# TensorE's instructions of both attention pipelines stay in the program's order

## The chip, the cores and the metric

The kernel runs on one core of a Trainium2 chip. The metric is the device time of one execution in microseconds (us). Five engines share the work: TensorE (PE, matmuls; PEld is its weight load), VectorE (DVE), ScalarE (ACT), GpSimd (POOL) and SyncE (SP, which issues most of the transfers).

## What is computed

Two layers of a hybrid backbone over 512 latent and 256 context tokens, model width 1024, all in float32. Each layer's mixer has three branches, merged by gates and projected:

```python
y_f = fourier_mix(f)
y_na = neighbourhood_attention(q, k, v, k_ctx, v_ctx, rpb, n_rows)   # 8 heads of 64, window 8 x 16 and all context keys
y_mla = blocked_attend(mla_q, mla_k, mla_v, MLA_SCALE)               # 8 heads, keys of 64 + 32, latent and context keys
out = merge_branches([y_f, y_na, y_mla], g, lp['w_branch'], lp['w_out'])
...
x = layer_norm(alpha * x + (1 + gate) * mix)
x = layer_norm(alpha * x + (1 + gate) * swiglu(adaLN(x)))
```

Context tokens attend to context alone, and in the second layer their outputs are not needed, so that layer's attention has queries of the latent tokens only.

## The kernel before

Every float32 product is made of three fp32r matmuls on a high and a low part of the operands (high by high, high by low, low by high; the names whi/wlo, AH/AL, kh/kl, mkh/mkl, mqh/mql). The program is a list of Steps; `drive()` (L182) runs them in order, splitting weights ahead of their use on ScalarE (L220) and GpSimd or VectorE (L221). A scheduler then reorders the instructions of each engine by its own estimate of the times, within the data dependencies. A step whose `pin` is set is exempt on TensorE: `order()` (L268) makes each of its TensorE instructions depend on the one before it in the program, with no semaphore. Some steps outside attention were pinned already: the merge's projection (L1717), the output norm (L1831 to L1848) and a part of the FFN (L1998).

Attention is done in units: one head pair by 128 queries. `na_unit` (L1149) is one of neighbourhood attention, `mla_unit` (L1482) one of latent attention. A unit has four parts:

- scores: the products of queries and keys into PSUM (NA L1190 to L1194, MLA L279), the row maximum on VectorE (NA L1203, L1204; MLA L1510, L1518, L1519, L1522) and the exponentials on ScalarE (NA L1206, L1207, L1210; MLA L1520, L1523);
- transposes: the weights p or mp are transposed on TensorE (NA L1228, MLA L1541, L1546) and copied to SBUF as pT or mpT (ScalarE L1230, L1232, L1542; VectorE L1548);
- norm: one over the sums, spread over columns, made once for two units (VectorE L1061, L1063, L1065), then transposed on TensorE (L1072);
- values: weights by values for two units at once, column-tiled: the two heads' instructions use different 64 columns of the array (NA L1244, L1252, MLA L1560), 12 instructions in a block for latent queries, 4 for context queries. VectorE scales the result (L1255, L1563).

`pipeline()` (L1114) writes the units out as a software pipeline. Its step `first` for unit n holds the norm of unit n-1, the scores of unit n and the values of unit n-2; its step `second` holds the transposes of unit n-1. Between them `weave()` (L130) puts fill by a hand-given cost: the next head pair's q and k projections, chunks of the branch gates (L287, computed ahead; tanh on ScalarE L1597, stored by L1598), in layer 0 blocks of the modulation product (L542, also column-tiled), and steps of the latent-attention prelude (L335). Neighbourhood attention runs it from `attention()` (L1262), latent attention from `mla_main()` (L1381), whose first steps also compute the values of the latent branch (L279 with vm, ScalarE copy L1409). The query's rotary part is split through a buffer of which there is one: qrh (ScalarE L1457), then mql (VectorE L1458).

At the end of layer 0's latent attention, VectorE starts sums of the merge (L444, L448) while the last units still run.

Of the kernel before, what the change touches and what calls it, by code (L numbers as in the profile page):

```python
# [108 lines left out]
def pinned(steps):  # L109

    for s in steps:
        s.pin = True
    return steps
# [16 lines left out]
def weave(main, fill):  # L130

    tm, tf = sum(s.cost for s in main), sum(s.cost for s in fill)
    out, cm, cf, j = [], 0.0, 0.0, 0
    for s in main:
        out.append(s)
        cm += s.cost
        while j < len(fill) and (cf + fill[j].cost / 2) * tm <= cm * tf:
            cf += fill[j].cost
            out.append(fill[j])
            j += 1  # L140
    return out + fill[j:]


class Kern:
# [969 lines left out]
    def pipeline(self, groups, fills, begin=()):  # L1114

        units = [u for g in groups for u in g]
        N = len(units)
        out, n = [], 0  # L1120
        for k, g in enumerate(groups):
            main = []
            for _ in range(len(g) + (2 if k == len(groups) - 1 else 0)):
                def first(ws, n=n):
                    if 0 <= n - 1 < N:
                        units[n - 1]["norm"]()
                    if n < N:
                        units[n]["scores"]()
                    if 0 <= n - 2 < N:
                        units[n - 2]["values"]()  # L1130

                def second(ws, n=n):
                    if 0 <= n - 1 < N:
                        units[n - 1]["transpose"]()

                c1 = (units[n]["c"][0] if n < N else 0) + (units[n - 2]["c"][2] if 0 <= n - 2 < N else 0)
                c2 = units[n - 1]["c"][1] if 0 <= n - 1 < N else 0
                gap = TAIL if n >= N else 0.0
                main += [Step(first, [], c1 + gap + 0.01), Step(second, [], c2 + gap + 0.01)]
                n += 1  # L1140
            first, spread = fills[k]
            c = PIPE_C if first else 0
            head = []
            if k == 0 and begin:
                head, main = weave(main[:4], begin), main[4:]
            out += weave(head + weave(main[:len(main) - c], first) + main[len(main) - c:], spread)
        return out

    def na_unit(self, l, hp, i, sh):  # L1149

# [1089 lines left out]
```

## Time and profile before

| | |
|---|---|
| median of 3 runs | 2359.95 us (2350.79 to 2362.65) |
| the profiled execution | 2358.29 us |
| its span | 2356.5 us |
| mean granted TensorE clock | 0.986 |
| TensorE busy | 2268.2 us (96%) |
| VectorE, ScalarE, GpSimd busy | 55%, 47%, 39% |
| layer 0: NA pipeline, then MLA pipeline | about 158 to 330, 367 to 532 us |
| layer 1: NA pipeline, then MLA pipeline | about 1487 to 1612, 1650 to 1778 us |

Times in rows are microseconds from the start of the span. In a timeline row stand the start, the length, the engine, the line and operation, the result and its operands, the shape and the count; in brackets the engine's idle time ahead of the row and what ended it. Lengths of matmuls overlap, so TensorE's pace is read from start to next start. The granted clock is a share of TensorE's full clock.

### The profile page before, as it was taken

To read this page: it belongs to the slowest core of one execution; us is meant where nothing else is said; L and a number is where in the kernel's file an instruction comes from. 1 tells how busy PE (TensorE), PEld (TensorE's weight loads), DVE (VectorE), ACT (ScalarE), POOL (GpSimd) and SP (SyncE) were. 2 spreads that over 40 slices of the span, in tenths; PEclk is the share of its full clock that TensorE was granted. 3 is DMA by queue.
4 is the path that set the end of the run, shared out by engine and by line. 5 is a ranking of instruction groups with operands and counts; after the bars stand their busy time and mean duration, and the time that the engine had idled before them with its cause. 6 is when DMAs were issued, how large, how long until landed. Compare 5 with 4: busy or idle time off the path is not lost. (4 is left out here: it accounts for less than half of the span.)

```text
span 2356.5 us, 36360 instructions
## 1 busy us (share of the span) xinstructions
PE 2268.2 (96%) x13806; PEld 1966.3 (83%) x13806; DVE 1291.3 (55%) x2404; ACT 1099.2 (47%) x2435; POOL 920.5 (39%) x684
## 2 busy tenths in 40 slices
PE   7999999999999999999999999999999999999997
PEld 5877788878998889999987888787778877999875
DVE  6334556655424487556532272445578257888544
ACT  5435666644421254444441253675675325554532
POOL 1232153102248534334348362325301773323483
PEclk9999999999999999999999999999999999999998
DMA  8465331117576432232162342222224844322342
GB/s 331 140 222 199 137 105 62 68 59 257 205 275 236 141 135 81 101 101 86 63 243 73 109 157 83 74 90 100 79 74 176 298 153 141 112 102 97 113 147 63
DMA packets 113467, 323.43 MB, mean 137 GB/s; under 512 B 12967, under 2 KB 24173, under 8 KB 113293
## 3 DMA queue, kind: packets, MB, share of 16 engines
q1 hardware_dynamic: 89900, 269.34, 33.2%
q10 hardware_dynamic: 20160, 46.49, 5.2%
q0 software_dynamic: 3232, 5.28, 0.8%
q8 instruction: 108, 1.77, 0.3%
q14 instruction: 67, 0.54, 0.1%
HBM read 269.92 MB, written 55.35 MB: 138 GB/s over the span
## 5 line engine op out<-in xcount | busy, mean ns | idle before, releaser
L221 POOL TENSOR_TENSOR wlo<-raw,whi 128x512 fp32r<-128x512 f32 (+2 forms) x413 | 573.9, 1397 | 918.7 <-ACT whi L220 856.3
L220 ACT CAST whi<-raw 128x512 fp32r<-128x512 f32 (+1 forms) x449 | 274.1, 616 | 442.3 <-PE ps L1698 83.7
L519 PE MATMUL ps<-tp,whi 128*128 128x384 f32 (+1 forms) x1088 | 267.3, 315 | 1.0 <-DVE tp L454 0.8
L519 PE MATMUL ps<-AH,whi 128*128 128x384 f32 (+1 forms) x628 | 196.8, 315 | 7.4 <-DVE hx L500 4.2
L287 PE MATMUL ps<-AH,whi 128*128 128x512 f32 (+1 forms) x616 | 195.4, 364 | 3.6 <-ACT AH L738 3.5
L519 PE MATMUL ps<-AH,wlo 128*128 128x384 f32 (+1 forms) x628 | 196.3, 313 | 0.0
L519 PE MATMUL ps<-AL,whi 128*128 128x384 f32 (+1 forms) x628 | 194.8, 312 | 0.0
L519 PEld LDWEIGHTS ps<-tp,whi 128*128 128x128 f32 x1088 | 190.6, 189 | 3.4 <-DVE tp L454 1.7
L287 PE MATMUL ps<-AH,wlo 128*128 128x512 f32 (+1 forms) x616 | 190.7, 358 | 0.0
L287 PE MATMUL ps<-AL,whi 128*128 128x512 f32 (+1 forms) x616 | 189.5, 357 | 0.0
L519 PE MATMUL ps<-tp,wlo 128*128 128x384 f32 (+1 forms) x544 | 171.0, 314 | 0.6 <-DVE wlo L221 0.6
L2052 PE MATMUL ps<-whi,hx 128*128 128x512 f32 x520 | 163.9, 394 | 7.6 <-DVE hx L2045 3.3
L335 PE MATMUL ps<-wlo,AH 128*128 128x512 f32 (+1 forms) x352 | 135.4, 385 | 0.8 <-POOL wlo L221 0.8
L335 PE MATMUL ps<-whi,AH 128*128 128x512 f32 (+1 forms) x352 | 134.2, 388 | 1.6 <-ACT whi L220 1.6
L335 PE MATMUL ps<-whi,AL 128*128 128x512 f32 (+1 forms) x352 | 135.4, 385 | 0.0
L287 PEld LDWEIGHTS ps<-AH,whi 128*128 128x128 f32 x616 | 105.9, 192 | 27.8 <-issue 7.7
L519 PEld LDWEIGHTS ps<-AH,whi 128*128 128x128 f32 x628 | 118.8, 190 | 11.6 <-DVE hx L500 5.1
L2052 PEld LDWEIGHTS ps<-whi,hx 128*128 128x128 f32 x520 | 98.8, 190 | 30.4 <-DVE hx L2045 3.8
L287 PEld LDWEIGHTS ps<-AL,whi 128*128 128x128 f32 x616 | 104.1, 190 | 20.1 <-issue 2.0
L519 PEld LDWEIGHTS ps<-AH,wlo 128*128 128x128 f32 x628 | 119.1, 190 | 0.3
L287 PEld LDWEIGHTS ps<-AH,wlo 128*128 128x128 f32 x616 | 104.7, 191 | 17.4 <-issue 1.5
L519 PEld LDWEIGHTS ps<-AL,whi 128*128 128x128 f32 x628 | 119.0, 190 | 0.0
(338 smaller groups left out, 5535.5 us busy)
## 6 DMA issues: line engine op xcount, KB each, us to landing
mraw<-in_w_mod_dram SPq DMA_DIRECT2D x80, 512.0 KB
raw<-in_w_down_dram SPq DMA_DIRECT2D x44, 512.0 KB
raw<-in_w_g_dram SPq DMA_DIRECT2D x42, 512.0 KB
raw<-in_w_up_dram SPq DMA_DIRECT2D x36, 512.0 KB
raw<-in_w_gate_dram SPq DMA_DIRECT2D x26, 512.0 KB
raw<-in_w_br_dram SPq DMA_DIRECT2D x24, 512.0 KB
gb<-th ACTq DMA_DIRECT2D x24, 384.0 KB
th<-gb SPq DMA_DIRECT2D x24, 384.0 KB
```

The lines of the kernel that those rows point to most:

```text
L220: hi_eng(hi[:, :n], x)
L221: lo_eng.tensor_sub(lo[:, :n], x, hi[:, :n].bitcast(F32))
L287: self.nc.tensor.matmul(ps, w.at(wt, ws), at[:, k0 + kc, cols], start=kc == 0 and i == 0, stop=kc == nk - 1 and i == 2)
L335: self.nc.tensor.matmul(ps, a[:, k0 + kc, tok], w.at(b, ws), start=kc == 0 and i == 0, stop=kc == 2 * nb - 1 and i == 2)
L519: nc.tensor.matmul(ps, ws[0].at(wt, w), act[at], start=new and kc == 0 and i == 0, stop=kc == 3 and i == 2, skip_group_check=True)
L2052: nc.tensor.matmul(ps, h[a][:, tok], w.at(b, ws), start=f == seq[0] and i == 0, stop=f == NF - 1 and i == 2)
```

## The change

All steps that `pipeline()` returns, the fill included, are pinned:

```diff
@@ -1144,7 +1144,7 @@
             if k == 0 and begin:
                 head, main = weave(main[:4], begin), main[4:]
             out += weave(head + weave(main[:len(main) - c], first) + main[len(main) - c:], spread)
-        return out
+        return pinned(out)
```

with

```python
def pinned(steps):

    for s in steps:
        s.pin = True
    return steps
```

The scheduler may no longer reorder TensorE's instructions there; the other engines' it may, and it does, since its estimate of the times changes with TensorE's order. What TensorE computes is the same. Up to the first NA pipeline of layer 0 the order on TensorE is the old one. Three places in which it isn't follow.

The first is on TensorE, near the end of layer 1's MLA pipeline: the last scores of a unit (mkh, mkl by mqh, mql), the values block of the pair before (L1560) and the transposes of mp (L1541, L1546). x12 is a count of instructions; a line with - stands in the old order, with + in the new.

```order
 L279 MATMUL ps_17794<-mkh_3261_16372,mqh_3491_17272 128x512
 L279 MATMUL ps_17794<-mkh_3261_16372,mql_3493_17274 128x512
 L279 MATMUL ps_17794<-mkl_3265_16376,mqh_3491_17272 128x512
-L1560 MATMUL ps_17814<-mpT_17689,vm_15704 64x256
+L1560 MATMUL ps_17814<-mpT_17689,vm_15704 64x256 x12
 L1541 MATMUL ps_17829<-ident,mp_17732 128x128 x4
-L1560 MATMUL ps_17814<-mpT_17689,vm_15704 64x256 x11
 L1541 MATMUL ps_17835<-ident,mp_17739 128x128 x4
 L1546 MATMUL ps_17841<-ident,mp_17732 128x128 x2
```

In the old order the block's first instruction stands alone, with four transposes between it and the other eleven; in the new one the twelve stand together.

The second is on TensorE at the end of layer 0's MLA pipeline: transposes, the norm's transpose (L1072), the last scores (ps_5870), the last full values block (L1560, ps_5887) and gate matmuls (L287, ps_5779 and ps_5780). One piece of the difference:

```order
-L287 MATMUL ps_5779<-AH,whi_5585 128x512
-L287 MATMUL ps_5780<-AH,whi_5585 128x256
-L287 MATMUL ps_5779<-AH,wlo_5586 128x512
-L287 MATMUL ps_5780<-AH,wlo_5586 128x256
-L287 MATMUL ps_5779<-AL,whi_5585 128x512
 L1546 MATMUL ps_5860<-ident,mp_5741 128x128 x2
 L1546 MATMUL ps_5860<-ident,mp_5748 128x128 x2
 L1072 MATMUL ps_5866<-ident,rw_5828 128x128 x2
-L287 MATMUL ps_5780<-AL,whi_5585 128x256
-L287 MATMUL ps_5779<-AH,whi_5585 128x512
 L279 MATMUL ps_5870<-mkh_821_3974,mqh_1105_5125 128x256
```

Seven gate matmuls leave the place ahead of the scores; in the new order they stand behind the values block, which is whole there and was cut into 8 and 4.

The third is the start of layer 1's MLA pipeline, on TensorE and on ScalarE. ps_16557, ps_16561 and ps_16568 are the first unit's scores, whi_16505 by CH and CL the product for vm. TensorE before:

```order
L279 MATMUL ps_16557<-mkh_3258_16369,mqh_3284_16451 128x256
L279 MATMUL ps_16561<-mkh_3258_16369,mqh_3284_16451 128x512
L279 MATMUL ps_16568<-mkh_3259_16370,mqh_3285_16452 128x512
L279 MATMUL ps_16598<-whi_16505,CH_15702 128x512
L279 MATMUL ps_16598<-whi_16505,CL_15703 128x512
```

and now:

```order
L279 MATMUL ps_16557<-mkh_3258_16369,mqh_3284_16451 128x256
L279 MATMUL ps_16557<-mkh_3258_16369,mql_3286_16453 128x256
L279 MATMUL ps_16557<-mkl_3262_16373,mqh_3284_16451 128x256
L279 MATMUL ps_16561<-mkh_3258_16369,mqh_3284_16451 128x512
L279 MATMUL ps_16561<-mkh_3258_16369,mql_3286_16453 128x512
```

Before, the products with mqh alone came first, then the values' product and gate work, and those with mql some 35 instructions later; now all of a unit's scores stand together. ScalarE at the same place before:

```order
L1452 CAST mqh_3353_16730<-qr_3266_16377 32x512
L1409 COPY vm_15704<-ps_16598 128x512
L1409 COPY vm_15704<-ps_16603 128x512
L1409 COPY vm_15704<-ps_16608 128x512
L1457 CAST qrh_16458<-qr_3266_16377 32x512
```

and now:

```order
L1452 CAST mqh_3353_16730<-qr_3266_16377 32x512
L1457 CAST qrh_16458<-qr_3266_16377 32x512
L1597 ACTIVATE th_16502<-ps_16477 128x512
L1598 DMA gb_136<-th_16502 128x512
L1457 CAST qrh_16464<-qr_3266_16377 32x512
```

The casts to qrh, which lead to mql, have moved ahead of the three copies to vm.

## The prediction

> **What bounds the kernel now.** First the page's busy times, then busy time by stretches for the two attention regions: layer 0 (150 to 535 us) and layer 1 (1480 to 1780 us).
>
> ```profile
> PE 2268.2 (96%) x13806; PEld 1966.3 (83%) x13806; DVE 1291.3 (55%) x2404; ACT 1099.2 (47%) x2435; POOL 920.5 (39%) x684
> ```
>
> ```profile
> 150.00:535.00 385.00, 373.29 (x2616) 298.32 (x2615) 218.01 (x529) 226.25 (x637) 102.54 (x86) 0.99 0.34 118
> 1480.00:1780.00 300.00, 287.40 (x1785) 233.52 (x1785) 165.44 (x398) 191.64 (x524) 93.72 (x86) 0.98 0.26 89
> ```
>
> Columns of the second view: the stretch, its length, busy time and instructions of PE, PEld, DVE, ACT and POOL, the granted TensorE clock, DMA share, GB/s. TensorE is the bound. In the two regions that the change touches it is idle for 385.00 - 373.29 = 11.7 us and 300.00 - 287.40 = 12.6 us, 24.3 us together. So the change can act in three ways only: through these 24.3 us, through new idle time, or through TensorE's own pace. TensorE's list of waits (total, times, longest) begins with the largest hole.
>
> ```profile
> PE ps L1072 <- DVE rw L1065: 7.8, 5, 5.1
> ```
>
> One wait of 5.1 us, at the end of layer 0's MLA pipeline, and one of 3.8 us at the start of layer 1's (its row is in part 3) make more than a third of the 24.3 us.
>
> **Part 1: values blocks are no longer cut.** The instruction counts stay; what goes is that the scheduler cut a block of column-tiled matmuls (L1244, L1252, L1560, L542) and put other matmuls between. TensorE's timeline shows a whole block and a cut one (each instruction leaves two rows in the trace; those of the two heads alternate and run side by side):
>
> ```profile
> 1686.50 2.81 PE L1560 MATMUL ps<-mpT,vm 128*64 128x256 f32 x24
> 1689.24 1.09 PE L1541 MATMUL ps<-ident,mp 128*128 128x128 f32 x8
> ...
> 1763.05 0.65 PE L1560 MATMUL ps<-mpT,vm 128*64 128x256 f32 x2
> 1763.63 0.66 PE L1541 MATMUL ps<-ident,mp 128*128 128x128 f32 x4
> 1764.21 2.80 PE L1560 MATMUL ps<-mpT,vm 128*64 128x256 f32 x22
> 1766.95 0.66 PE L1541 MATMUL ps<-ident,mp 128*128 128x128 f32 x4
> ```
>
> Start to next start, the whole block takes 1689.24 - 1686.50 = 2.74 us. The cut one takes (1763.63 - 1763.05) + (1766.95 - 1764.21) = 0.58 + 2.74 = 3.32 us: the lone first instruction costs 0.58, since its neighbour of the other head isn't beside it. The four transposes ahead of the second piece take 0.58 us, those behind it 0.49: another 0.09. A cut of this kind costs 0.67 us.
>
> A cut in the middle is cheaper:
>
> ```profile
> 474.19 1.95 PE L1560 MATMUL ps<-mpT,vm 128*64 128x256 f32 x16
> 476.07 0.44 PE L1546 MATMUL ps<-ident,mp 128*128 128x128 f32 x2
> ...
> 477.25 1.08 PE L1560 MATMUL ps<-mpT,vm 128*64 128x256 f32 x8
> 478.27 0.44 PE L1546 MATMUL ps<-ident,mp 128*128 128x128 f32 x2
> ```
>
> 1.88 + 1.02 = 2.90 us against 2.74, and 0.09 for the second way in: 0.25 us. Before, 11 blocks are cut after their first instruction (8 of L1244, 3 of L1560), four in the middle, and one modulation block (L542) in three places, costed as a first cut and two middle ones, 0.67 + 0.5, about 1.1 us. After, none is cut. Gross: 11 x 0.67 + 4 x 0.25 + 1.1 = 9.5 us.
>
> Not all of it is a gain. A cut lets TensorE work on while ScalarE copies the second half of the block's operand. Where that copy is late, the uncut block waits instead. One row from TensorE, then two of ScalarE:
>
> ```profile
> 199.16 0.65 PE L1244 MATMUL ps<-pT,vc 128*64 128x256 f32 x2
> ```
>
> ```profile
> 199.94 0.28 ACT L1232 COPY pT<-ps 64x128 f32<-64x128 f32 x1
> ...
> 1759.96 0.60 ACT L1542 COPY mpT<-ps 128x512 f32<-128x512 f32 x1
> ```
>
> At 199 us the copy ends at 200.2, 1.0 us behind the block's start, and the second instruction, of the other head, needs it: the uncut block waits about 0.9 us, for 0.67 saved. At 1763 us it had ended at 1760.56: the saving is clean. Three NA blocks of layer 0 are of the first kind; I book -0.3 us each, -1.0 in all (0 to -2.7). A fourth, in layer 1's first NA pair, goes with part 4. The other seven are clean: 7 x 0.67 = 4.7. Of the middle cuts three count (0.8); the fourth lies ahead of the 5.1-us wait and is hidden in it. With the modulation block's 1.1, **part 1 is +4.7 + 0.8 + 1.1 - 1.0 = +5.6 us** (range 0 to 9.5).
>
> **Part 2: end of layer 0's MLA.** Seven gate matmuls move from ahead of the last scores to behind the last values. First TensorE, then VectorE:
>
> ```profile
> 510.14 0.60 PE L287 MATMUL ps<-AH,whi 128*128 128x512 f32 x2
> ...
> 511.16 0.60 PE L1546 MATMUL ps<-ident,mp 128*128 128x128 f32 x4
> ...
> 511.73 0.36 PE L287 MATMUL ps<-AL,whi 128*128 128x256 f32 x1
> ...
> 512.17 0.28 PE L279 MATMUL ps<-mkh,mqh 96*128 96x256 f32 x1
> ```
>
> ```profile
> 513.08 0.69 DVE L1510 TENSOR_REDUCE mmc<-ps 128x2 f32<-128x512 f32 x1 [0.59 <-PE ps L279]
> 513.68 4.76 DVE L444 TENSOR_TENSOR t<-AH,AL 128x384 f32<-128x384 f32 x10
> ```
>
> From the scores' maximum (L1510) on VectorE has no gap until the copy L1065, which ends the 5.1-us wait: ten L444 of the merge come first, alone 4.76 us, and the order is the same after the change but for one L448. So L1065 moves with those scores, and they come (511.16 - 510.14) + (512.17 - 511.73) = 1.5 us earlier. TensorE's own work is unchanged, so the wait falls from 5.1 to about 3.7 us and what follows starts 1.4 us earlier. **+1.4 us** (0 to 1.5; zero if the L444 are not yet released so early).
>
> **Part 3: start of layer 1's MLA.** Before, ready matmuls stand between the pieces of the first scores, whose operand mql is late. After, the scores stand whole, and TensorE waits for mql. ScalarE, VectorE, TensorE:
>
> ```profile
> 1652.51 1.94 ACT L1409 COPY vm<-ps 128x512 f32<-128x512 f32 x3
> 1654.47 0.62 ACT L1457 CAST qrh<-qr 32x512 fp32r<-32x512 f32 x1
> ```
>
> ```profile
> 1655.12 0.68 DVE L1458 TENSOR_TENSOR mql<-qr,qrh 32x512 fp32r<-32x512 f32 x1 [2.43 <-ACT qrh L1457]
> ```
>
> ```profile
> 1650.62 1.14 PE L279 MATMUL ps<-mkh,mqh 96*128 96x256 f32 x3
> ...
> 1666.87 2.24 PE L1541 MATMUL ps<-ident,mp 128*128 128x128 f32 x8 [3.81 <-ACT mp L1520]
> ```
>
> In the new order of ScalarE, L1457 stands ahead of the three L1409, so it can start at 1652.51, and L1458 ends near 1652.51 + 0.62 + 0.07 + 0.68 = 1653.9. TensorE, there since 1651.0, waits 2.9 us. The second head goes through the same one-buffer qrh behind it: about 1655.3, a further 0.4 us. Then 12 us of scores, values and gate work run through, and the exponentials of L1520, whose scores are complete at 1655.9 and not at 1663.06, are long done: the 3.81-us wait goes. Transposes start at 1650.6 + 12.4 of work + 3.3 = 1666.3 rather than 1666.87. They also run at full clock: before, the granted clock was 0.50 from 1666.9 to 1671.5 (the second row of the last fence below), so those 4.6 us of work take 2.3. Gain 0.6 + 2.3 = 2.9 us if the new wait leaves the clock alone.
>
> Does it? The nearest rows: two waits, then the clock behind each, with the stretch of 1666.9 between:
>
> ```profile
> 1287.03 0.50 PE L2052 MATMUL ps<-whi,hx 128*128 128x512 f32 x1 [2.94 <-DVE t L1786]
> 1968.49 0.58 PE L296 MATMUL ps<-AL,whi 128*128 128x256 f32 x1 [1.47 <-POOL AL L403]
> ```
>
> ```profile
> 1287.00:1290.40 3.40, 3.37 (x14) 2.51 (x15) 3.40 (x6) 0.00 (x0) 0.00 (x0) 1.00 0.35 125
> 1666.90:1671.50 4.60, 4.59 (x17) 3.70 (x18) 0.62 (x4) 4.60 (x17) 0.00 (x0) 0.50 0.00 0
> 1968.50:1972.00 3.50, 3.50 (x16) 3.38 (x16) 2.60 (x5) 1.21 (x2) 3.31 (x2) 0.52 0.96 315
> ```
>
> A 2.94-us wait cost no clock, one of 1.47 us cost half a clock for 3.5 us, that is 1.7 us of work. So I take half of 1.7 off: **+2.0 us** (1.2 to 2.9). The Trainium skill, "TensorE: Matmul & The Clock Gate", section "Why this matters for your kernels", advises against idle gaps over about 3 us; by that the 2.9-us wait would be free and this part +2.9. The 1.47-us row disagrees, so the sum doesn't use it.
>
> **Part 4: smaller places.** Start of layer 0's MLA: one late key operand now holds TensorE for about 1.4 us, against a wait of 0.5 and some reordering recovered: -0.6. Start of layer 1's NA pipeline: the first unit's transposes stand ahead of 12 gate matmuls (2.8 us), so TensorE waits some 3 us for exponentials which it spent on them before; the four later waits there (0.3, 1.0, 0.8, 0.4) and one of 0.8 go, since the gate work is then still in hand: 0 (-2 to +0.6). Two later NA head pairs of layer 1 put values right behind scores and gate work last: a new wait near 1.4 us against a wait of 0.9 on L1065 that goes: -0.5 each, **-1.6 us in all** (-4 to +1).
>
> **Sum.** 5.6 + 1.4 + 2.0 - 1.6 = +7.4 us, so 2358.29 (the profiled execution: span 2356.5 and 1.8 us around it) becomes 2351. That run is 1.7 us under the median, 2359.95, of three that reach from 2350.79 to 2362.65; on the median's footing 2352.5. I forecast **2352 us**, 0.3% less. A measurement of this kernel can tell about 0.5%, 11.8 us, from no change.
>
> **Rivals.**
> **Stalls at the head of the line (slower).** Any late operand now stops all of TensorE's attention work, with ready gate and projection matmuls queued behind it. For: the three NA places above (0.9 us each); ScalarE carries 226 us of work in 385, and NA units have 3 to 4 us of cover. Against: whole blocks already run without a wait at most units, and only 24.3 us are idle in both regions. There are 40 values blocks in the program; if 20 of them, the NA ones, wait 0.9 us each, that is 18 us, and two waits that halve the clock add 3.4: 2352 + 21 = about 2373. It decides from some 20 us of new idle time on. Chance 0.17.
> **The two big waits vanish (faster).** If the new order also feeds softmax sooner, so that half of the 24.3 us goes, and the cuts give their whole 9.5 us: 2358.3 - 12 - 9.5 = 2337. Against: the 5.1-us wait hangs on VectorE's L444, which nobody moves. Chance 0.27 for more than 0.5%.
> **Nothing comes of it.** The rows do move, so the change does what it says; but what TensorE saves ahead of a VectorE- or ScalarE-bound wait is given back there, as with the fourth middle cut: 2356 to 2360. This lies within the same band as the forecast, 0.56 together: own range 2348 to 2363.
>
> **Numbers.** Low end: the faster rival, 2337. High end: part 1 to 4 at their poor ends (0 + 0 + 1.2 - 4 = -3, 2361) and a third of the stalls rival, 7 us: 2368. Faster 0.27, same 0.56, slower 0.17.
>
> **What would show it.** Right: no L1560 or L1244 block of x2 and x22 rows; the wait of L1072 near 525 us under 4 us; no wait of L1541 on L1520 in layer 1, in its place one of L279 on L1458 of near 3 us. Wrong: a list of waits in which L1228, L1244, L1541 or L1560 wait on ScalarE more than some 10 us in all, or a granted clock that is at half in the NA stretches.

## The result, and the profile after

Over seven runs of each the changed kernel takes 2371.7 us (2366.69 to 2376.98) against 2359.95 us; the ratio is 1.0051, 95% interval 1.0035 to 1.0067. It is about 0.5% slower, 12 us, where 2352 us were forecast. The profiled execution took 2372.9 us, with a span of 2371.1 us and a granted clock of 0.985. Its busy times on the page:

```profile
PE 2260.5 (95%) x13806; PEld 1967.8 (83%) x13806; DVE 1288.9 (54%) x2404; ACT 1100.3 (46%) x2435; POOL 916.0 (39%) x684
```

TensorE is busy for 7.7 us less than before and the span is 14.6 us longer, so the loss is waiting. Busy time by stretches, in the changed kernel, for the same two regions as in the prediction:

```profile
150.00:535.00 385.00, 366.52 (x2607) 298.18 (x2606) 217.50 (x528) 226.51 (x637) 101.26 (x86) 0.99 0.33 116
1480.00:1780.00 300.00, 282.27 (x1754) 232.19 (x1753) 160.80 (x396) 190.00 (x520) 91.02 (x84) 0.97 0.26 86
```

Idle time is 18.5 us in the first (11.7 before) and 17.7 us in the second (12.6 before): 11.9 us more.

**Layer 0.** TensorE's timeline at the first scores of neighbourhood attention, its last values block, and the last values of latent attention, before:

```profile
160.12 0.58 PE L1190 MATMUL ps<-kh,qs 128*128 128x256 f32 x1
...
327.50 1.08 PE L1244 MATMUL ps<-pT,vc 128*64 128x256 f32 x8
...
531.02 1.08 PE L1560 MATMUL ps<-mpT,vm 128*64 128x256 f32 x8
```

and after:

```profile
159.19 0.39 PE L1190 MATMUL ps<-kh,qs 128*128 128x256 f32 x1
...
322.30 1.08 PE L1244 MATMUL ps<-pT,vc 128*64 128x256 f32 x8
...
531.98 1.08 PE L1560 MATMUL ps<-mpT,vm 128*64 128x256 f32 x8
```

The NA pipeline went from 167.4 to 163.1 us, 4.3 us shorter; the MLA pipeline behind it from 203.5 to 209.7 us, 6.2 us longer. TensorE's list of waits in this part (325 to 535 us; total, times, longest), after:

```profile
PE ps L1072 <- DVE rw L1065: 5.4, 2, 4.5
PE ps L279 <- DVE mql L1449: 1.6, 1, 1.6
PE ps L1541 <- ACT mpT L1542: 1.4, 2, 0.7
PE ps L279 <- DVE mkl L1469: 1.2, 1, 1.2
...
PE ps L1546 <- ACT mpT L1542: 0.7, 1, 0.7
```

Before, the same list had the 5.1 us of L1072 and one more wait within attention, of 0.5 us:

```profile
PE ps L1541 <- ACT mp L1520: 0.5, 1, 0.5
```

The new ones are the scores of the first and the third unit, which stand whole and wait for their late operands (mkl, mql: 2.8 us), three transposes that wait for ScalarE's copies of earlier ones (2.1 us) and a second, short wait of L1072 (0.9). That is 5.8 us; the longest wait of L1072, now 4.5, gives 0.6 back and the old one of 0.5 is gone, so 4.7 of the 6.2 us are waits. The rest is about what the clock cost. Behind the 1.6-us wait of L279 the granted clock was 0.50 for 3.41 us, 1.7 us of work; in the kernel before it was 1.00 at this place. After:

```profile
385.93:389.34 3.41, 3.41 (x16) 3.25 (x16) 1.99 (x5) 3.13 (x9) 0.00 (x0) 0.50 0.00 0
```

**Layer 1, end of latent attention.** TensorE before, then after:

```profile
1770.68 0.60 PE L1541 MATMUL ps<-ident,mp 128*128 128x128 f32 x4
1771.04 0.48 PE L287 MATMUL ps<-AH,whi 128*128 128x512 f32 x1
...
1772.75 0.60 PE L1541 MATMUL ps<-ident,mp 128*128 128x128 f32 x4
1773.19 0.60 PE L1546 MATMUL ps<-ident,mp 128*128 128x128 f32 x4
1773.55 0.47 PE L287 MATMUL ps<-AH,wlo 128*128 128x512 f32 x1
...
1774.80 0.42 PE L1072 MATMUL ps<-ident,rw 128*128 128x128 f32 x2
1775.14 2.81 PE L1560 MATMUL ps<-mpT,vm 128*64 128x256 f32 x24
1777.88 0.50 PE L287 MATMUL ps<-AH,whi 128*128 128x512 f32 x1
```

```profile
1769.34 1.04 PE L1541 MATMUL ps<-ident,mp 128*128 128x128 f32 x8
1770.22 0.60 PE L1546 MATMUL ps<-ident,mp 128*128 128x128 f32 x4
1774.79 0.44 PE L1072 MATMUL ps<-ident,rw 128*128 128x128 f32 x2 [3.97 <-DVE rw L1065]
1775.15 4.48 PE L1560 MATMUL ps<-mpT,vm 128*64 128x256 f32 x24
1779.56 0.51 PE L287 MATMUL ps<-AH,whi 128*128 128x512 f32 x1
```

L1072, the norm's transpose, starts at the same moment in both (1774.8), since VectorE's L1065, behind sums of the merge, ends no sooner (before, then after):

```profile
1774.43 0.28 DVE L1065 COPY rw<-srec 128x256 f32<-128x256 f32 x1
```

```profile
1774.44 0.28 DVE L1065 COPY rw<-srec 128x256 f32<-128x256 f32 x1
```

Before, twelve gate matmuls (L287) stood here and filled the time: seven between the last transposes and five behind them, ahead of L1072. In the program's order the twelve stand behind the values block. TensorE comes to the last transposes 1.3 us earlier than before (1769.34 against 1770.68) and has nothing ready behind them: it waits 3.97 us, and the block L1560 behind the wait takes 1779.56 - 1775.15 = 4.41 us instead of 2.74. That is 5.6 us of a place that cost nothing before; 1.3 us of it is the lead that TensorE had.

Behind it, in the merge, VectorE's first L454 comes later as well. VectorE before, then after:

```profile
1784.73 1.43 DVE L454 TENSOR_TENSOR tp<-t,tp 128x256 fp32r<-128x256 f32 x4 [2.87 <-ACT tp L453]
```

```profile
1789.92 0.43 DVE L454 TENSOR_TENSOR tp<-t,tp 128x256 fp32r<-128x256 f32 x1 [7.77 <-DMA yl<-yb]
```

Its wait grew from 2.87 to 7.77 us, with a transfer as the last to arrive. From the merge's first projection (L519) to its output projection (L335) the profile has 4.0 us more than before. Behind that it has 6.2 us more and between the layers 3.1 us less. Both vary widely in the 17 profiles (439.6 to 454.2 us and 953.1 to 961.6 us), so no cause is read from them here.

**Layer 1, neighbourhood attention.** The forecast wait at its start is there too. Behind it the clock is at half for 6.83 us. After:

```profile
1490.74 0.87 PE L1228 MATMUL ps<-ident,p 128*128 128x128 f32 x4 [3.09 <-ACT p L1206]
```

```profile
1491.85:1498.68 6.83, 6.05 (x17) 4.72 (x18) 1.44 (x6) 4.09 (x17) 0.00 (x0) 0.50 0.00 0
```

This pipeline took 123.1 us, 1.5 us more than before.

**Layer 1, start of latent attention.** The forecast wait is there, and what the clock did behind it (TensorE's timeline, then the stretches behind that row), after:

```profile
1652.35 0.58 PE L279 MATMUL ps<-mkh,mql 96*128 96x256 f32 x1 [3.14 <-DVE mql L1458]
```

```profile
1652.35:1655.50 3.15, 3.15 (x10) 2.76 (x11) 2.00 (x3) 1.22 (x2) 2.77 (x2) 0.50 0.87 225
1655.50:1658.70 3.20, 3.20 (x8) 2.43 (x8) 1.99 (x5) 1.78 (x4) 0.00 (x0) 0.50 0.50 168
```

For these 6.35 us the granted clock is 0.50, and it stays there until 1659.11: 6.8 us, that is 3.4 us of work lost.

### The profile page after: what moved, and what is told of

Its sections match the earlier page's. It is cut to its first block, busy times and chain, and to the rows that moved or that the text cites. A ratio compares the mean times of both kernels' runs of the same rounds, so it can differ in the third digit from the quotient of the medians.

```text
span 2371.1 us, 36341 instructions
## 1 busy us (share of the span) xinstructions
PE 2260.5 (95%) x13806; PEld 1967.8 (83%) x13806; DVE 1288.9 (54%) x2404; ACT 1100.3 (46%) x2435; POOL 916.0 (39%) x684
## 5 line engine op out<-in xcount | busy, mean ns | idle before, releaser
L519 PE MATMUL ps<-tp,whi 128*128 128x384 f32 (+1 forms) x1088 | 267.8, 316 | 1.6 <-DVE tp L454 0.8
L519 PE MATMUL ps<-AH,whi 128*128 128x384 f32 (+1 forms) x628 | 195.3, 314 | 5.7 <-DVE hx L500 3.1
L519 PE MATMUL ps<-AH,wlo 128*128 128x384 f32 (+1 forms) x628 | 195.5, 312 | 1.8 <-POOL wlo L221 1.8
L287 PE MATMUL ps<-AH,whi 128*128 128x512 f32 (+1 forms) x616 | 191.9, 366 | 3.6 <-ACT AH L738 3.5
L519 PEld LDWEIGHTS ps<-tp,whi 128*128 128x128 f32 x1088 | 191.3, 190 | 4.2 <-DVE tp L454 1.6
L519 PE MATMUL ps<-AL,whi 128*128 128x384 f32 (+1 forms) x628 | 193.8, 311 | 0.0
L287 PE MATMUL ps<-AH,wlo 128*128 128x512 f32 (+1 forms) x616 | 186.2, 357 | 0.0
L287 PE MATMUL ps<-AL,whi 128*128 128x512 f32 (+1 forms) x616 | 185.6, 356 | 0.0
L519 PE MATMUL ps<-tp,wlo 128*128 128x384 f32 (+1 forms) x544 | 171.5, 315 | 0.7 <-POOL wlo L221 0.7
L335 PE MATMUL ps<-wlo,AH 128*128 128x512 f32 (+1 forms) x352 | 135.3, 384 | 3.1 <-POOL wlo L221 3.1
L335 PE MATMUL ps<-whi,AH 128*128 128x512 f32 (+1 forms) x352 | 134.3, 389 | 2.1 <-ACT whi L220 2.1
L335 PE MATMUL ps<-whi,AL 128*128 128x512 f32 (+1 forms) x352 | 135.0, 384 | 0.0
L287 PEld LDWEIGHTS ps<-AH,whi 128*128 128x128 f32 x616 | 103.8, 192 | 30.1 <-issue 9.8
L519 PEld LDWEIGHTS ps<-AH,whi 128*128 128x128 f32 x628 | 118.2, 189 | 9.1 <-DVE hx L500 3.8
L519 PEld LDWEIGHTS ps<-AH,wlo 128*128 128x128 f32 x628 | 118.4, 189 | 2.5 <-POOL wlo L221 2.0
L519 PEld LDWEIGHTS ps<-AL,whi 128*128 128x128 f32 x628 | 118.2, 189 | 0.0
L287 PEld LDWEIGHTS ps<-AL,whi 128*128 128x128 f32 x616 | 102.5, 190 | 18.9 <-issue 0.8
L287 PEld LDWEIGHTS ps<-AH,wlo 128*128 128x128 f32 x616 | 103.5, 192 | 16.7
```

What stands on the lines that cost most here:

```text
L287: self.nc.tensor.matmul(ps, w.at(wt, ws), at[:, k0 + kc, cols], start=kc == 0 and i == 0, stop=kc == nk - 1 and i == 2)
L335: self.nc.tensor.matmul(ps, a[:, k0 + kc, tok], w.at(b, ws), start=kc == 0 and i == 0, stop=kc == 2 * nb - 1 and i == 2)
L519: nc.tensor.matmul(ps, ws[0].at(wt, w), act[at], start=new and kc == 0 and i == 0, stop=kc == 3 and i == 2, skip_group_check=True)
```

## The experiments

Theory after the result: a pinned order is paid at a few places, where a step that waits for another engine has lost the ready work that stood ahead of it; these are layer 0's MLA pipeline and the end of layer 1's. Rivals: the price is spread over all units; it comes from the order behind the pipelines (the merge's order changes too); or whole blocks save nothing. The kernels differ from the changed one in what pipeline() pins. They note their place with `self.where = (l, 'na')` or `(l, 'mla')` ahead of the call. All ratios are to the kernel before, with 95% intervals. Single executions of one kernel differ by up to 22 us (2349 to 2371 us in 35 of the kernel before), so the ratio is taken as the time, and of a single profile only the length of a stage is used.

**Which pipeline.** Four kernels, one line each:

```diff
-        return pinned(out)
+        return pinned(out) if self.where != (1, 'mla') else out      # e1_all_but_last
+        return pinned(out) if self.where == (1, 'mla') else out      # e2_last_only
+        return pinned(out) if self.where[0] == 0 else out            # e3_layer0_only
+        return pinned(out) if self.where[1] == 'na' else out         # e4_na_only
```

> Three of the four pipelines are pinned; layer 1's latent attention is free, and from there on TensorE's order is that of before. Theory A (the loss is made at the end of layer 1's latent attention, by a 4.0-us wait of L1072 and what it delays): no loss, 2354 to 2360 us, ratio 0.997 to 1.001, and no wait of L1072 near 1775 us. Theory B (late operands stop TensorE at many units): most of the loss stays, some three quarters of 12 us, ratio 1.003 to 1.005.

> Only layer 1's latent attention is pinned; up to it TensorE's order is that of before. Theory A: the whole loss, 2368 to 2376 us, ratio 1.004 to 1.007, with the 4-us wait of L1072 near 1775 us. Theory B: a quarter of it, ratio 1.000 to 1.002.

> Both pipelines of layer 0 are pinned, neither of layer 1; TensorE's order from layer 0's merge on is that of before. Theory A: the place of L1072 at the end of layer 0 is 0.7 us later in the trace of the change, so ratio 0.999 to 1.002. Theory B: half the loss, about 1.0025. The prediction's sum for layer 0 (clean blocks, the modulation block, part 2, the late key) would be about -6 us, 0.997.

> Only the neighbourhood attention of both layers is pinned. In the trace of the change layer 0's part gained 5.0 us at 323 us and layer 1's lost about 0.1. Theory A: these 5 us come through, 2352 to 2356 us, ratio 0.997 to 0.9985. A third theory (C: whatever is gained early is given back at the next place where VectorE sets the time): ratio 1.000. Theory B: slower, 1.002.

| kept in order | ratio | interval |
|---|---|---|
| all but layer 1's MLA | 1.0011 | 0.9995 to 1.0027 |
| layer 1's MLA alone | 1.0041 | 1.0023 to 1.0059 |
| layer 0 alone | 1.0009 | 0.9994 to 1.0024 |
| NA of both layers | 0.9985 | 0.9971 to 0.9998 |

Neighbourhood attention is where the change gains (3.5 us), so the price isn't spread over its units; layer 1's MLA is the dearest place. Theory A fits all four (the first by a hair), but it names only the end of layer 1: with NA's gain in them, 1.0011 and 1.0009 leave a second price in layer 0. In layer 0's NA the nine profiles in which it is pinned are 0.9 to 4.3 us shorter than before, mean 2.8 (where it isn't, from 1.3 shorter to 0.3 longer). In layer 0's MLA the profiles with that pipeline pinned are 5.5 to 7.4 us longer, the others between 0.3 shorter and 1.9 longer. Layer 1's NA is 0.1 to 1.5 us longer in the eight profiles in which it is pinned; the four with 1.3 or more are those in which the clock was at half for 6.83 us behind the 3.1-us wait.

**The end of layer 1's MLA.** The last eight steps of that pipeline freed (e6), or alone pinned (e10):

```diff
-        return pinned(out)
+        return pinned(out[:-8]) + out[-8:] if self.where == (1, 'mla') else pinned(out)      # e6_free_tail
+        return out[:-8] + pinned(out[-8:]) if self.where == (1, 'mla') else out              # e10_last_8_steps
```

> The change, with only the last 8 steps of layer 1's latent pipeline left free: the order of TensorE at its end and in the merge is that of before, in the FFN it is not. Theory A: the 4-us wait near 1775 us and its half clock go, and the merge starts 5 to 8 us earlier, ratio 1.0015 to 1.003 (layer 0's MLA loss of some 5 us stays). Theory D (new order in merge and FFN): the FFN's part of 3 us or so stays as well, ratio 1.003 to 1.0045.

> Only the last 8 steps of layer 1's latent pipeline are pinned; TensorE's order is that of before up to there, the merge has the new order. If the wait of L1072 with its half clock (5.7 us) and the merge's order (about 5) are the whole loss of the change: 9 to 12 us, ratio 1.004 to 1.005. Theory A without the merge: 1.0025. Theory B (many units): below 1.001.

e6: 1.0013 (0.9996 to 1.0031), that is 0.4% less than with these steps pinned. e10: 1.0016 (1.0002 to 1.0030), where 1.004 to 1.005 was forecast if this place were the whole loss and 1.0025 for its wait alone. (The medians of e10 and of the kernel before, 2366.9 and 2360.9 us, are 6.0 us apart, more than the ratio's 3.8.) TensorE's timeline of e10 has the wait and the slow block with nothing else pinned:

```profile
1774.33 0.60 PE L1546 MATMUL ps<-ident,mp 128*128 128x128 f32 x4
1778.89 0.69 PE L1072 MATMUL ps<-ident,rw 128*128 128x128 f32 x2 [3.97 <-DVE rw L1065]
1779.51 5.14 PE L1560 MATMUL ps<-mpT,vm 128*64 128x256 f32 x24
```

Eight steps suffice for the 3.97-us wait and the slow block. Two more kernels keep the order but move the norm's transpose of the last pair from behind the transposes to the head of its values, and set more fill ahead of it: with everything pinned and in both layers (e5), and on top of e10 (e11, layer 1 alone):

```diff
-TAIL = 2.5
+TAIL = 2.5; LATE_C = 9.0
...
-                c2 = units[n - 1]["c"][1] if 0 <= n - 1 < N else 0
+                c2 = (units[n - 1]["c"][1] if 0 <= n - 1 < N else 0) + (LATE_C if n == N and self.where[1] == 'mla' else 0)
...
-            if u == 1:
+            if u == 1 and not (hp == 3 and i == nq - 1):
                 self.scale_rows(sh["w"])
...
-            y = self.ps()
+            (self.scale_rows(sh["w"]) if hp == 3 and i == nq - 1 else None); y = self.ps()
```

> All four pipelines pinned as in the change, but at the end of both latent pipelines the norm's transpose (L1072) of the last pair goes from behind its transposes to the head of its values block, and fill stands between: 12 gate matmuls in layer 1, 48 in layer 0 (of which 24 stood there). Theory A (head-of-line waits of L1072 at the two ends): waits of 4.0 and 4.5 us and the half clock behind each go, some 6 us per layer, ratio 0.999 to 1.001. Theory D (the loss is the scheduler's new order in the merge and FFN of layer 1, which changes here too but differently): waits go, yet the ratio stays above 1.003.

> As the run before, but with the norm's transpose at the head of the last values block and 12 gate matmuls ahead of it, so that the wait falls from 4.0 to about 1.1 us and keeps full clock; the merge has the new order as well. Theory A: ratio 1.000 to 1.001. Theory D: the merge's part stays, 1.002 to 1.003.

e11: 1.0007 (0.9994 to 1.0021). On TensorE the hole is gone:

```profile
1770.02 0.40 PE L287 MATMUL ps<-AL,whi 128*128 128x512 f32 x1
1770.71 0.41 PE L1072 MATMUL ps<-ident,rw 128*128 128x128 f32 x2 [0.30 <-DVE rw L1065]
```

So the wait was a matter of what stands ahead of L1072. But VectorE's late L454 remains in e11:

```profile
1784.20 0.42 DVE L454 TENSOR_TENSOR tp<-t,tp 128x256 fp32r<-128x256 f32 x1 [7.82 <-DMA xraw<-in_w_g_dram]
```

and from the first to the output projection of the merge its profile is 4.5 us longer than before. The late L454 is therefore not a result of the 3.97-us wait. It stands in every kernel with these eight steps pinned (after, e2, e5, e10, e11) and in none of the others. The transfer that its row names differs (yl, xraw, gb), but all five have one thing in common: the store of the last gate that latent attention computes (L1598). The twelve matmuls behind the values block are the last of that gate, so its store is issued late. ScalarE before, then after:

```profile
1775.62 0.33 ACTq L1598 DMA_DIRECT2D gb<-th  x1
```

```profile
1783.30 0.33 ACTq L1598 DMA_DIRECT2D gb<-th  x1
1789.86 1.33 ACT L453 CAST tp<-t 128x256 fp32r<-128x256 f32 x4 [0.95 <-DMA gb<-th]
```

In the five traces L454 waits for the semaphore of this store, and starts 0.22 us behind its last update each time (1789.70 and 1789.92 in the changed kernel); in the other twelve traces the first L454 waits for ScalarE alone. So gate matmuls that stand behind the values block cause both the hole on TensorE and the late L454 on VectorE. In e11 twelve earlier ones fill the hole, but the last twelve still stand behind the block, and the store stays late. What ties L454 to the store, a buffer that is used again perhaps, isn't shown. Nor is it shown that a late L454 makes the merge longer. The merge takes 1.8 to 7.2 us more in these five profiles and within 0.8 us of before in all others but one: e7 below, whose L454 isn't late, has 3.8 us more. e10 and e11 differ by less than their intervals, so how the price splits between the wait and L454 isn't measured either.

e5 measured 1.0043 (1.0023 to 1.0062): a miss. It takes the hole at layer 1's end away, and its ratio can't be told from the 1.0051 of the change. Its profile is that of its fastest execution and doesn't show where the median's time goes. The record gives the granted clock of every execution: on the mean 0.9852 in e5 and 0.9878 in the executions of the kernel before that ran alongside. A clock lower by 0.0026 over 2355 us is 6 of e5's 10 us; why it is lower stays open.

**Cuts, and the order behind.** Four kernels change the order within the values blocks, so that fewer are cut though MLA isn't pinned: e7 pins nothing and reverses all blocks (46 pieces instead of 55), e8 pins NA on top of it, e12 pins NA and reverses layer 0's MLA blocks alone. e9 pins nothing and reverses one block, the last of layer 1's MLA, which moves little in attention but gives TensorE another order in the merge.

```diff
-                for j in range(2):
+                for j in (1, 0):                         # e7 and e8, L1244 and L1252
...
-            for a, c in enumerate(cl):
-                for j in range(2):
+            for a, c in enumerate(reversed(cl)):         # e7, e8: all; e12: l == 0; e9: l == 1 and hp == 3 and i == 3
+                for j in (1, 0):
```

> No pipeline is pinned. Inside each values block the operand that is copied last is used first (second head first, chunks backwards in latent attention), so that the scheduler starts a block only when it can run through: 46 runs of values in place of 55, where 40 would be none cut. This is part 1 of the prediction nearly alone. The prediction's price of a cut, 0.67 us for a lone first instruction and 0.25 for a middle one: 3 to 6 us gained, ratio 0.9975 to 0.9988. If cuts cost nothing in sum: 1.000.

> Neighbourhood attention of both layers pinned (the run of that alone: 0.9985), and latent attention free with its blocks kept together through the operands' order (22 runs of L1560 in place of 27). If the two gains add: ratio 0.996 to 0.998; if what is gained ahead of the end of layer 0's latent attention is lost in its 5-us wait: 0.9985 again.

> Nothing is pinned. Only the last values block of layer 1's latent attention takes its operands in reverse; that block stands whole before and after, and TensorE's order is that of before up to its end and again in the FFN. In between, in layer 1's merge, the scheduler makes of it the same new order as in the change. Theory D (the new order of the merge costs by itself): 3 to 7 us, ratio 1.0015 to 1.003. Theory A (only the wait of L1072 costs): 1.000.

> Neighbourhood attention pinned in both layers, and in layer 0's latent attention the values blocks take their operands in reverse, so that fewer are cut; the merge keeps the order of before. As the run with neighbourhood attention pinned alone (0.9985), or 1 to 2 us better: 0.9975 to 0.9985. If that run's gain was chance: 0.9995 to 1.0005.

| kernel | ratio | interval |
|---|---|---|
| e7, blocks reversed, nothing pinned | 1.0007 | 0.9989 to 1.0025 |
| e8, the same with NA pinned | 1.0009 | 0.9992 to 1.0026 |
| e9, merge order alone | 0.9992 | 0.9981 to 1.0003 |
| e12, NA pinned, layer 0's MLA reversed | 0.9987 | 0.9977 to 0.9996 |

e9 takes most of the second rival away: the other order of the merge on TensorE alone costs nothing. e7 shows no gain from fewer cuts, and e12's is that of e4. e8 is a miss: 0.9985 or less was forecast, and even the gain of NA in order isn't there. Its mean clock was lower too, 0.9858 against 0.9878, which is 4.7 us; why isn't known. Fewer cuts by themselves didn't show in a time, for which the few microseconds at stake may be too small.

**Both places at once.** These three were run to see whether the two places are the whole loss. e13 pins everything but them, e14 the first alone, e15 layer 1's MLA without its end:

```diff
-        return pinned(out)
+        return (out if self.where == (0, 'mla') else
+                pinned(out[:-8]) + out[-8:] if self.where == (1, 'mla') else pinned(out))    # e13_bar_two_places
+        return pinned(out) if self.where == (0, 'mla') else out                              # e14_layer0_mla_only
+        return pinned(out[:-8]) + out[-8:] if self.where == (1, 'mla') else out              # e15_layer1_mla_bar_end
```

> Everything stays in the program's order but the two places to which the runs so far lead: layer 0's MLA and the last 8 steps of layer 1's MLA are free. Theory (the two places are the whole loss): what is left is layer 0's NA, -2.9 us, and the start of layer 1's MLA, -1.9 us, less at most 1.6 us inside layer 1's MLA, so some 3 to 5 us faster, ratio 0.998 to 0.9987; transposes of layer 1's MLA start about 2 us earlier, and the merge starts no later than before. Rival (the loss is spread over all that is pinned, or comes from the order further back): slower than before, 1.001 or more.

> Layer 0's MLA alone stays in the program's order. Theory: that pipeline takes 5 to 7 us longer in the profile, with new waits of PE on the key and query operands of its first scores, on ScalarE's copies mpT and a wait of L1072 that is still above 4 us; ratio 1.002 to 1.003. Rival (only the merge of layer 1 costs; what layer 0 loses is made up behind it): 1.000 to 1.001.

> Layer 1's MLA alone stays in the program's order, but for its last 8 steps. Theory (the end is what costs there): the ratio falls from 1.0041 of the run with the end to about 1.000 (0.999 to 1.001), with the transposes at the start some 2 us earlier and VectorE no longer idle for over 5 us ahead of its first L454. Rival (the remainder of the 1.0041 comes from the pipeline's middle or from the order of the layers behind it): 1.003 or more.

| kernel | ratio | interval | us of 2358.36 |
|---|---|---|---|
| e13 | 0.9979 | 0.9965 to 0.9993 | -5.0 |
| e14 | 1.0031 | 1.0017 to 1.0044 | +7.3 |
| e15 | 0.9998 | 0.9983 to 1.0014 | -0.5 |

e14's list of TensorE's waits from 325 to 535 us repeats that of the changed kernel: the four rows of L279, L1541 and L1546 shown there are the same to the digit, and the first is

```profile
PE ps L1072 <- DVE rw L1065: 5.3, 2, 4.5
```

e15 (TensorE, then VectorE) has neither the hole nor the late L454:

```profile
1771.13 0.44 PE L1072 MATMUL ps<-ident,rw 128*128 128x128 f32 x2 [0.42 <-DVE rw L1065]
1771.50 2.81 PE L1560 MATMUL ps<-mpT,vm 128*64 128x256 f32 x24
```

```profile
1781.38 1.43 DVE L454 TENSOR_TENSOR tp<-t,tp 128x256 fp32r<-128x256 f32 x4 [3.17 <-ACT tp L453]
```

The pipelines add up: NA alone -0.0015 (e4), layer 0's MLA alone +0.0031 (e14) and layer 1's MLA alone +0.0041 (e2) make +0.0057, against +0.0051 for the change. Within layer 1's MLA the last eight steps carry the price: from e2 to e15, which differ in them alone, the ratio falls by 0.0043, some 10 us. By themselves (e10) they cost 3.8 us, or 6.0 by the medians; whether the price depends on what is pinned ahead of them isn't settled. With e14's 7.3 us the two places make 11 to 17 us. From the changed kernel to e13, where both are free, the ratio falls by 0.0072, 17 us. e13 is faster than both kernels: 0.2% under the one before, 0.7% under the changed one (0.9979 / 1.0051 = 0.993).

The ratios of e14 and e15 came as expected. In e15 the transposes at the start of layer 1's MLA are 2.5 us earlier, of which 0.9 us was left at the merge. In e13, with the same order there, they are only 0.2 us earlier: the clock was at half for 3.41 us on the way (from 1627.3 us), as it was before (from 1630.6 us) but not in e15, so 1.7 of e15's 2.5 us are the clock's. Most of what e13's profile gains lies behind the merge, where it spends 3.4 us at half clock and the profile of before 20.5 us (the last 20 us of the span left out). Over all executions e13's clock was not the higher one (0.987 against 0.988), so the 5.0 us are no gift of the clock; but where all of them come from isn't shown.

## Why the prediction was wrong

**Part 1 (no cut blocks), +5.6: right in size in layer 0's NA, not shown elsewhere.** There it had three clean first cuts, the modulation block and the three late ones: 3 x 0.67 + 1.1 - 1.0 = +2.1. Measured: 2.8 us on the mean; how much of it is the cuts was not measured apart. The late blocks do wait, and little, in the changed kernel's list of waits over the whole span (before: 1.8, 3, 0.8):

```profile
PE ps L1244 <- ACT pT L1230: 2.3, 5, 0.5
```

The remaining cuts lie in the MLA pipelines and in layer 1's NA, where larger terms cover them, and e7 doesn't show them by themselves.

**Part 2 (end of layer 0's MLA), +1.4: right in kind, too large.** The wait of L1072 fell from 5.1 to 4.50 us, not to 3.7:

```profile
525.88 0.69 PE L1072 MATMUL ps<-ident,rw 128*128 128x128 f32 x2 [4.50 <-DVE rw L1065]
```

VectorE's order moved a little as well: from the start of the last L1510 to that of L1065 it took 12.1 us instead of 11.7.

**Part 3 (start of layer 1's MLA), +2.0: the rows were right, the clock wasn't.** The 2.9-us wait came as 3.14, the 3.81-us wait of L1541 went, and the transposes started earlier. But the clock was booked at half of 1.7 us and cost 3.4 us, the stretch at 0.50 shown above. In e15, which has this part without the end, 0.9 us of gain is left by the merge, in e6 0.2. The Trainium skill, "TensorE: Matmul & The Clock Gate", section "Why this matters for your kernels", advises against idle gaps over about 3 us. The three new waits above that in attention, 3.09, 3.14 and 3.97 us, were all followed by a slow stretch, and so far the traces agree with it. But one followed the wait of 1.6 us in layer 0's MLA as well; what the clock goes by here is in the last section.

**Part 4 (smaller places), -1.6: this is the step that failed.** "Start of layer 0's MLA ... -0.6" took one late operand and no more. There were two, 2.8 us, a half clock behind the second (1.7 us), and later transposes that wait for ScalarE's copies (2.1 us); with part 2's smaller gain the pipeline takes some 6 us longer (e14: 7.3 in the ratio), where parts 1, 2 and 4 together had it some 3 us shorter. And the end of layer 1's MLA is in no part at all. Part 2 looked at layer 0's end, where VectorE's sums already made a wait of 5.1 us; at layer 1's the same VectorE sums stood behind a wait that the gate matmuls filled, so the list of waits had no row for it. What the list of waits doesn't show is what the old order hid. The two places are the 11 to 17 us of the last experiments. The part's guess for layer 1's NA, some 3 us of new wait and 1.0 us in all, was fair: 3.09 us, and 0.1 to 1.5 us in all.

**The rivals.** "Stalls at the head of the line" was the true one in kind and in time (2373 forecast, 2371.7 measured), with a chance of 0.17, and wrong in place, so its hit on the time is luck: it priced 20 NA units at 0.9 us. NA gained. The stalls that cost are in latent attention, they are few, and the dearest hangs on VectorE, not on ScalarE. So the first sign that was named for "wrong", waits of L1228, L1244, L1541 or L1560 on ScalarE of over 10 us, didn't show (7.8 us, against 8.2 before); the waits were those of L1072 and L279 on VectorE. The second sign, a clock at half in the NA stretches, did, in layer 1. The rival's other half, two waits that halve the clock, happened four times (behind new waits of 1.6, 3.09, 3.14 and 3.97 us). Slow stretches of the kernel before went in exchange, so over the whole span the granted clock only moved from 0.986 to 0.985. The range ended at 2368 us because only a third of this rival was let into it.

**What stays open:** whether the late L454 lengthens the merge, what ties it to the gate's store, why the last eight steps cost 3.8 us by themselves and some 10 us with the rest of the pipeline pinned, the lower clock of e5 and e8, and where all of e13's gain comes from.

## What to carry to other kernels

Before an order is fixed, list each step in it that waits for another engine, at the end of each pipeline too, and look at what stood ahead of it in the free order: ready work there is cover that no list of waits shows, and it is lost if the fixed order has it behind. Look also at what hangs on the work that moves: here a store, and on it another engine's work in the next stage. Fix the order by place, not all at once: here neighbourhood attention gains from it, layer 0's latent attention and the last eight steps of layer 1's lose, and leaving those two free turned 0.5% slower into 0.2% faster.

## What the runs showed of the hardware

The length of a wait doesn't tell what it costs in clock. In every trace here the granted clock is either full or half, and from 100 us to 40 us before the end it changes only at points that lie 3.41 us apart, on one grid per execution. Take the slots between these points in all 17 profiles. Where the clock was full and TensorE was busy for less than 40% of a slot, the next slot was at half clock: 88 of 88. From 40 to 58% both happened (72 of 133 went to half). At 58% or more it never did (0 of 10582). A slot at half clock that was busy for less than 80% was followed by another (44 of 44).

So it is the slot that counts, not the wait: a wait is dear if it falls into one slot, or if other idle time falls there too (layer 0's 1.6 us: 1.55 us busy of 3.41), and can be cheap if the edge of a slot divides it. The prediction's wait of 2.94 us, which cost nothing, was divided: TensorE was busy for 1.69 and 2.20 us of the two slots (before). The wait of 3.14 us fell into one slot, with 0.34 us busy, and two slots at half clock followed (after):

```profile
1282.40:1285.81 3.41, 1.69 (x8) 1.06 (x6) 0.00 (x0) 0.00 (x0) 2.84 (x3) 1.00 0.87 279
1285.81:1289.23 3.42, 2.20 (x10) 1.83 (x11) 2.95 (x5) 0.00 (x0) 0.00 (x0) 1.00 0.64 181
```

```profile
1648.87:1652.28 3.41, 0.34 (x1) 0.14 (x1) 2.10 (x4) 2.98 (x5) 3.41 (x4) 1.00 0.18 58
1652.28:1659.11 6.83, 6.76 (x18) 5.53 (x19) 4.01 (x8) 3.42 (x7) 2.84 (x2) 0.50 0.63 182
```

Where the grid lies differs from execution to execution. After the same wait of 3.97 us the half clock lasted 3.41 us in the changed kernel and 6.83 us in e10, and the 24 rows of L1560 took 4.48 and 5.14 us, against 2.81 us without a wait. Much of the scatter between executions of one kernel goes with this: in the kernel before, one execution took 2350.27 us at a mean clock of 0.991 and one 2366.79 us at 0.985, and 0.006 of 2355 us is 14 of these 16.5 us.
